# Stores of z, mixing, gated product and residual sums issued from GpSimd's queue instead of SyncE's, in a hybrid gMLP and state-space block

## The chip, the core and the metric

The kernel runs on one core of a Trainium2 chip. The metric is the device time of one execution in microseconds (us). The kernel before has a median of 2923.4 us over three runs (2920.72 to 2925.73 us).

The engines have the names of the profile: PE is TensorE (matrix products), DVE is VectorE, ACT is ScalarE, POOL is GpSimd, SP is SyncE, which computes nothing and only issues transfers. "SPq", "ACTq" and "POOLq" are rows for the instructions that an engine's sequencer carries out itself: transfers that it issues, and waits. Every engine works through its own list of instructions in order. An instruction that waits for a semaphore holds back all that stand behind it on the same engine.

## The reference

One layer of a block for 2048 latent tokens of width 1024 (and 256 context tokens, which only supply the starting states of the scans), all in fp32:

```python
hl = _rms(x) * norm1_w * (1 + sc1) + sh1
proj = hl @ w_in                                  # u, v | z, xbc, dt
xs, bm, cm = split(silu(conv5(xbc)))
y = ssd_forward(xs, dt, bm, cm) + flip(ssd_backward(...))
g = (y + xs * d_skip) * silu(z)                   # z is used here
ssd_out = _rms(g per group) * ssd_norm_w
u, v = split(gelu(proj[..., :2048]))
mixed = einsum('hts,bcshd->bcthd', gm_ws, _rms(v)) + gm_bs
gm_out = u * mixed                                # the gated product
x = x + g1 * (concat(gm_out, ssd_out) @ w_out)    # the residual sums
x = x + g2 * swiglu(_rms(x) * norm2_w * (1 + sc2) + sh2)
return _rms(x) * final_norm_w
```

## The kernel before

Tokens are the free dimension in most places: a tile is 128 partitions x 512 tokens (256 KB), `TB = 512`, and two such tiles make a block `blk` of 1024 tokens. Every matrix product is split in three fp32r products (high x high, high x low, low x high; lines 234 to 236 in the projections, 1179 to 1181 and 1309 to 1311 in the feed-forward part, which forms each product from seven half-size ones). PE writes to PSUM; three PSUM banks (`mmp`) serve the large products in turn and five (`smp`) the small ones.

Results that don't fit in SBUF go to scratch tensors in DRAM and are loaded again later: `zscr` (z after SiLU), `mscr` (the mixing result), `gmscr` (the gated product), `x2scr` (the residual sums), `hscr` (states of the backward scan), `fscr` and `r3scr` (rows that are spread over the partitions when they are loaded), `sscr` (the scan's output), `cscr`, `ascr`, `wscr` (feed-forward). In SBUF most working tiles come from one ring of 14 buffers, `tma` (`NTMA`); from the last output half on, from a ring of 14, `t2`. Whoever writes a buffer next waits until its last readers are done, and a store is such a reader until its data has landed.

Stages, with their place in the span:

- 0 to 300 us: loads, modulation parameters, the conv branch of block 1 (`xbc(1, ...)`).
- 300 to 590 us: `run` at line 1024. The main generator is `proj_v(1)`, `proj_u(1)`, `proj_z(1)`; the second one runs states of the backward scan, row statistics and parameters beside it.
- 590 to 745 us: `xbc(0, ...)`.
- 745 to 1485 us: `run` at line 1033. The main generator is `proj_z(0)`, `proj_v(0)`, `proj_u(0)`, then `out_half(1, 0)`, `out_half(0, 0)`, `out_half(0, 1)`. The second is the rest of the backward scan and `ssd_y`, which forms the scan's output for 16 chunks x 2 groups, with `SIDE = 2.61` of its steps for one main step.
- 1485 to 1612 us: `out_half(1, 1)` beside `border()` (line 1350), which prepares the operands of the feed-forward part.
- From 1612 us: `ffn1` and `ffn2` for both blocks.

A main step is: the matrix products of one 128 x 512 result (`mm3`), then `flush()`, then a few DVE and ACT instructions that make the result from PSUM, and at the end `behind(dst, src)`, which only notes down the store. `flush()` of the next main step issues it (lines 578 to 585). So each store is issued one main step after its data was asked for, behind the loads that were issued in between. There are 160 of these stores, 32 each to `zscr`, `mscr` and `gmscr` and 64 to `x2scr`, each 128 x 512 fp32, and all are issued on SP by line 584, or rather by the queue of SyncE, `DMA = nc.sync` (line 87). SP also issues all loads. ACT issues the stores of `sscr`, `r3scr` (lines 834 and 848) and part of `rec`.

The producers of the stored tiles are DVE instructions: line 698 (z), 645 (mixing), 621 (gated product), 932 (residual sums). `V` is DVE, `S` ACT, `G` POOL (line 87).

`ssd_y` uses POOL. `y_seg` loads two rows spread over the partitions (`f_load`, lines 760 and 761), then ACT (782, 784, 786) and DVE (783, 785) make the decay matrices, POOL multiplies them (787) and forms `xd` (793). `y_out` has these lines, in which DVE waits for POOL twice:

```python
            G.tensor_tensor(out=h3(h), in0=h3(h), in1=hv(tot[:, c, g * 8:g * 8 + 8]), op=ALU.mult)
            V.tensor_tensor(out=h, in0=h, in1=pS, op=ALU.add)
        V.tensor_tensor(out=ya, in0=ya, in1=yb, op=ALU.add)
        V.tensor_tensor(out=ya, in0=ya, in1=py, op=ALU.add)
        G.tensor_tensor(out=h3(yb), in0=h3(rc[:, R_X:R_X + TB]), in1=hv(row[:, 64 + g * 8:64 + g * 8 + 8]), op=ALU.mult)
        V.tensor_tensor(out=ya, in0=ya, in1=yb, op=ALU.add)
```

(lines 813 to 818). Then z is loaded (822) and multiplied in (823). Before each output half, `load_mix` (line 883) loads 2 x 8 tiles for the next one; for the scan's half it loads `r3scr` rows (line 286) first and then scales and splits the tiles on DVE (895, 898) and ACT (897). After the last output half line 1360 calls `flush()` once more; the loads of the feed-forward operands (`hl_back`, line 1130) come next, and the splits of line 1064 and 1065. `border()` uses POOL for lines 1068.

Semaphores and the order of instructions within each engine are set by the framework from the code; the order it sets isn't always that of the code.

Of the kernel before, what the change touches and what calls it, by code (L numbers as in the profile page):

```python
# [83 lines left out]
def kernel(ctx: ExitStack, tc: tile.TileContext, xT, ctxp, cc, crow, wad1, wad2, vecs, rows,  # L84
                             gmb, wall, wdt, gmw, csts, outT, dbg=None):
    nc = tc.nc
    V, S, G, PE, DMA = nc.vector, nc.scalar, nc.gpsimd, nc.tensor, nc.sync
# [493 lines left out]

    def flush():
        for dst, src in pending:
            DMA.dma_start(dst, src)
        pending.clear()

    def gelu2(ps, mk):
# [19 lines left out]
    def proj_u(blk, hs):  # L607
        for h0 in range(0, 8, 2):
            us = [unit(U_U + h0), unit(U_U + h0 + 1)]
            for j in range(2):  # L610
                ts_ = slice((blk * 2 + j) * TB, (blk * 2 + j + 1) * TB)
                for i, (hi, lo) in enumerate(us):
                    m = tmp()
                    DMA.dma_start(m[:, :TB], mscr[h0 + i][:, ts_])
                    ps = mmp()
                    mm3(ps, [(hi[:, k * P:(k + 1) * P], lo[:, k * P:(k + 1) * P], hs[j][k][:, 0, :], hs[j][k][:, 1, :]) for k in range(KT)])
                    flush()
                    if tails and (j or i):
                        tails.pop(0)()
                    t = gelu2(ps, tmp)  # L620
                    V.tensor_tensor(out=t[:, :TB], in0=t[:, :TB], in1=m[:, :TB], op=ALU.mult)
                    behind(gmscr[h0 + i][:, ts_], t[:, :TB])
                    yield

    def proj_v(blk, hs):
# [25 lines left out]
        for hh in range(2):  # L651
            us = [unit(U_V + hh * 4 + i) for i in range(4)]
            for j in range(2):
                vh = []
                ms = sml()[:, :16]
                for c in range(4):
                    ps = mmp()
                    mm3(ps, stat_terms(hs, j * 4 + c, us, 0))
                    flush()
                    v = gelu2(ps, xin)  # L660
                    sq = tmp()
                    for h in range(4):
                        S.activation(sq[:, h * P:(h + 1) * P], v[:, h * P:(h + 1) * P], AF.Square, accum_out=ms[:, c * 4 + h:c * 4 + h + 1])
                    vh.append(v)
                    if prev is not None:
                        if c == 1:
                            gate_load(prev[0], 0)
                        if c >= 2:
                            mixing(*prev, 2 * c - 4)
                        if c == 2:  # L670
                            gate_load(prev[0], 2)
                    if c < 3:
                        yield
                V.tensor_scalar(out=ms, in0=ms, scalar1=1.0 / P, scalar2=4 * EPS, op0=ALU.mult, op1=ALU.add)
                r = newton(ms, 16)
                for c, v in enumerate(vh):
                    V.tensor_tensor(out=v[:, :TB].rearrange("p (a b) -> p a b", b=P), in0=v[:, :TB].rearrange("p (a b) -> p a b", b=P),
                                    in1=bc(r[:, c * 4:c * 4 + 4].rearrange("p (a o) -> p a o", o=1), P), op=ALU.mult)
                yield
                prev = (hh, j, vh)  # L680
# [7 lines left out]
    def proj_z(blk, hs):  # L688
        for g in range(2):
            us = [unit(U_Z + g * 4 + i) for i in range(4)]  # L690
            for c in range(8):
                ps = mmp()
                mm3(ps, stat_terms(hs, c, us, 0))
                flush()
                zdone[0] += 1 - blk
                t = tmp()
                S.activation(t[:, :TB], ps, AF.Tanh, scale=0.5)
                V.scalar_tensor_tensor(out=t[:, :TB], in0=t[:, :TB], scalar=1.0, in1=ps, op0=ALU.add, op1=ALU.mult)  # L698
                behind(zscr[blk * 8 + c][:, g * TB:(g + 1) * TB], t[:, :TB])
                yield  # L700
# [758 lines left out]
```

## Time and profile before

| | us |
|---|---|
| median of three runs | 2923.4 |
| lowest, highest | 2920.72, 2925.73 |
| the profiled execution | 2923.61 |
| its span, first to last instruction | 2921.8 |
| PE busy in the span | 2803.1 |
| DVE, ACT, POOL busy in the span | 1975.6, 1274.2, 645.4 |
| mean granted TensorE clock | 0.98 of full speed |

The span is cut in 40 slices on the page, and a digit gives the busy tenths of a slice. PEclk is the granted clock in the same way; of the two levels, 2.4 and 1.2 GHz, a 9 is all or nearly all time at the upper one. In the lists, "L584" is line 584. "A <- B: 82.2, 30, 8.2" in a list of waits says that A sat idle for 82.2 us in 30 waits that B ended, the longest 8.2 us. In a timeline the columns are start, duration, engine, line, operation and tiles, a count when several alike were merged, and in brackets the idle time of the engine just before and what ended it.

### The profile page before, as it was taken

What the parts mean: (1) busy time and instruction counts of PE and PEld (TensorE: products, weight loads), DVE (VectorE), ACT (ScalarE), POOL (GpSimd) and SP (SyncE); (2) the same over time, 40 slices, a digit from 0 to 9 for tenths busy, and PEclk for the clock granted to TensorE, in tenths of its full rate; (3) what the DMA queues carried; (4) which work ended last, traced back from release to release, by engine and by line L of the source; (5) the groups of instructions that cost most, each with busy time, mean ns of one, the idle gap of its engine ahead of it and who ended that gap; (6) DMA issues with size and microseconds to landing.
All of it is one profiled execution on the core that took longest, in us unless ns stands there. A gap on an engine that the chain in (4) does not pass through costs nothing. (4 is left out here: it accounts for less than half of the span.)

```text
span 2921.8 us, 36695 instructions
## 1 busy us (share of the span) xinstructions
PE 2803.1 (96%) x12478; PEld 2242.7 (77%) x12478; DVE 1975.6 (68%) x3007; ACT 1274.2 (44%) x2361; POOL 645.4 (22%) x555
## 2 busy tenths in 40 slices
PE   7999999999999998998979899999999999999997
PEld 2788778888677776776768688888887788888886
DVE  6776866886678888678676765555876544445556
ACT  4445343344356555444443533333554333333443
POOL 3200000200032233232202444444211222221000
PEclk8999999999999999999989999999999999999998
DMA  6232567743664678787658444445775423334654
GB/s 228 89 94 78 193 226 243 252 127 91 224 187 145 185 253 269 230 268 235 211 178 282 170 156 149 165 154 181 256 249 195 133 102 101 108 109 136 224 192 162
DMA packets 296743, 528.02 MB, mean 181 GB/s; under 512 B 28998, under 2 KB 89830, under 8 KB 296556
## 3 DMA queue, kind: packets, MB, share of 16 engines
q1 hardware_dynamic: 255756, 505.48, 53.0%
q10 hardware_dynamic: 40800, 20.21, 2.4%
q8 instruction: 98, 1.61, 0.2%
q14 instruction: 89, 0.73, 0.1%
HBM read 382.94 MB, written 142.64 MB: 180 GB/s over the span
## 5 line engine op out<-in xcount | busy, mean ns | idle before, releaser
L1065 DVE TENSOR_TENSOR hl<-w,hl 128x1024 fp32r<-128x1024 f32 x286 | 372.1, 1306 | 300.8 <-ACT hl L1064 129.5
L1064 ACT CAST hl<-w 128x1024 fp32r<-128x1024 f32 x286 | 298.8, 1048 | 423.1 <-PE smp L1311 150.0
L234 PE MATMUL mmp<-actt,whi 128*128 128x512 f32 x1120 | 455.7, 407 | 13.3 <-DVE tma L932 8.7
L236 PE MATMUL mmp<-actt,wlo 128*128 128x512 f32 x1120 | 442.1, 395 | 0.0
L235 PE MATMUL mmp<-actt,whi 128*128 128x512 f32 x1120 | 441.5, 394 | 0.2 <-DVE actt L898 0.2
L1179 PE MATMUL mmp<-hl,hl 128*128 128x512 f32 x704 | 276.5, 393 | 2.6 <-ACT t L1204 2.6
L1181 PE MATMUL mmp<-hl,hl 128*128 128x512 f32 x704 | 275.7, 392 | 1.0 <-DVE hl L1065 1.0
L1180 PE MATMUL mmp<-hl,hl 128*128 128x512 f32 x704 | 275.6, 392 | 0.0
L234 PEld LDWEIGHTS mmp<-actt,whi 128*128 128x128 f32 x1120 | 213.7, 191 | 62.0 <-DVE tma L932 9.7
L235 PEld LDWEIGHTS mmp<-actt,whi 128*128 128x128 f32 x1120 | 213.8, 191 | 47.0 <-issue 4.3
L236 PEld LDWEIGHTS mmp<-actt,wlo 128*128 128x128 f32 x1120 | 213.2, 190 | 46.0 <-issue 0.2
L234 PE MATMUL mmp<-whi,actt 128*128 128x512 f32 x512 | 208.9, 408 | 2.9 <-DVE tma L698 2.9
L1180 PE MATMUL smp<-hl,hl 128*128 128x512 f32 x528 | 208.5, 395 | 3.0 <-DVE hl L1065 3.0
L1181 PE MATMUL smp<-hl,hl 128*128 128x512 f32 x528 | 208.2, 394 | 2.5 <-DVE hl L1065 2.5
L1179 PE MATMUL smp<-hl,hl 128*128 128x512 f32 x528 | 209.8, 397 | 0.4 <-ACT hl L1064 0.4
L235 PE MATMUL mmp<-wlo,actt 128*128 128x512 f32 x512 | 206.4, 403 | 0.5 <-DVE wlo L221 0.5
L236 PE MATMUL mmp<-whi,actt 128*128 128x512 f32 x512 | 206.0, 402 | 0.0
L1071 DVE TENSOR_TENSOR t<-smp,t 128x512 f32<-128x512 f32 x88 | 60.5, 687 | 181.1 <-PE smp L1181 131.4
L787 POOL TENSOR_TENSOR tma<-tma 128x512 f32<-128x512 f32 x64 | 93.4, 1461 | 339.4 <-ACT tma L786 138.4
L456 DVE SCALAR_TENSOR_TENSOR tma<-xin,cw,tma 128x512 f32<-128x512 f32 x192 | 144.3, 751 | 25.5 <-ACT tma L454 19.3
L1179 PEld LDWEIGHTS mmp<-hl,hl 128*128 128x128 f32 x704 | 132.7, 189 | 32.5 <-ACT t L1204 3.0
L1071 POOL TENSOR_TENSOR w<-w 128x512 f32<-128x512 f32 x44 | 58.9, 1339 | 446.2 <-DVE hl L1065 290.8
(276 smaller groups left out, 5809.0 us busy)
## 6 DMA issues: line engine op xcount, KB each, us to landing
w<-in_wall_dram SPq DMA_DIRECT2D x110, 512.0 KB, 3.8
ws<-in_wall_dram SPq DMA_DIRECT2D x104, 512.0 KB, 5.0
ascr<-t SPq DMA_DIRECT2D x154, 256.0 KB, 3.9
w<-ascr SPq DMA_DIRECT2D x154, 256.0 KB, 3.3
tma<-fscr SPq DMA_DIRECT2D x128, 256.0 KB, 5.7
w<-wscr SPq DMA_DIRECT2D x88, 256.0 KB, 3.0
t<-x2scr SPq DMA_DIRECT2D x76, 256.0 KB, 4.1
w<-in_wall_dram SPq DMA_DIRECT2D x66, 256.0 KB, 3.1
```

The costliest lines, as they stand in the source:

```text
L234: PE.matmul(ps, lhsT=lh, rhs=rh, start=(i == 0), stop=False)
L235: PE.matmul(ps, lhsT=lh, rhs=rl, start=False, stop=False)
L236: PE.matmul(ps, lhsT=ll, rhs=rh, start=False, stop=(i == n - 1))
L456: V.scalar_tensor_tensor(out=acc[:, :n], in0=raw[:, j:j + n], scalar=cw[:, ch, j:j + 1], in1=acc[:, :n], op0=ALU.mult, op1=ALU.add)
L787: G.tensor_tensor(out=A, in0=A, in1=fb, op=ALU.mult)
L1064: S.copy(hi, x)
L1065: eng.tensor_tensor(out=lo, in0=x, in1=hi.bitcast(F32), op=ALU.subtract)
L1071: eng.tensor_tensor(out=o, in0=a, in1=b, op=ALU.add)
L1179: PE.matmul(ps, lhsT=hi[:, ms_], rhs=t[:, 0, :], start=first and k == 0, stop=False, skip_group_check=not first)
L1180: PE.matmul(ps, lhsT=hi[:, ms_], rhs=t[:, 1, :], start=False, stop=False, skip_group_check=not first)
L1181: PE.matmul(ps, lhsT=lo[:, ms_], rhs=t[:, 0, :], start=False, stop=k == 3, skip_group_check=not first)
```

## The change

In `flush()` the queue of POOL takes the place of that of SP. Nothing else is edited:

```diff
     def flush():
         for dst, src in pending:
-            DMA.dma_start(dst, src)
+            G.dma_start(dst, src)
         pending.clear()
```

`flush()` is called at lines 617 (`proj_u`), 659 (`proj_v`), 694 (`proj_z`), 931 (`out_half`) and 1360 (after the last output half). All 160 stores go through it.

## Rows read from the trace of the kernel before

**Rows 1.** The page: busy time by engine, and the granted clock in 40 slices.
```profile
PE 2803.1 (96%) x12478; PEld 2242.7 (77%) x12478; DVE 1975.6 (68%) x3007; ACT 1274.2 (44%) x2361; POOL 645.4 (22%) x555
...
PEclk8999999999999999999989999999999999999998
```

**Rows 2.** Busy time by stretch: length, PE, PEld, DVE, ACT, POOL, clock, DMA share, GB/s.
```profile
300.00:590.00 290.00, 285.16 (x1278) 229.00 (x1277) 222.36 (x428) 111.96 (x239) 16.02 (x17) 1.00 0.69 230
...
745.00:1485.00 740.00, 695.83 (x3124) 541.49 (x3125) 582.76 (x1148) 369.72 (x983) 203.23 (x156) 0.97 0.71 222
1485.00:1612.00 127.00, 116.35 (x499) 93.80 (x498) 85.68 (x132) 54.92 (x85) 17.33 (x12) 0.96 0.74 239
```

**Rows 3.** PE's instructions at its longest waits, from the timeline of PE.
```profile
1375.23 0.65 PE L831 MATMUL smp<-ident,tma 128*128 128x128 f32 x4 [3.82 <-DVE tma L823]
1387.59 2.04 PE L801 MATMUL smp<-h,rec_sb 128*128 128x512 f32 x2 [4.64 <-issue]
...
1522.64 0.79 PE L234 MATMUL mmp<-actt,whi 128*128 128x512 f32 x1 [8.72 <-DVE tma L932]
...
1634.83 0.50 PE L1181 MATMUL smp<-hl,hl 128*128 128x512 f32 x1 [2.53 <-DVE hl L1065]
```

**Rows 4.** SP's own waits over the whole span, those of the stores of line 584.
```profile
SPq L584 <- DVE tma L932: 82.2, 30, 8.2
...
SPq L584 <- DVE tma L621: 57.3, 23, 5.1
SPq L584 <- DVE tma L698: 56.9, 17, 8.4
```

**Rows 5.** Instructions of one line (584, 787, 793): count, duration min/median/max in ns.
```profile
L584 SPq DMA_DIRECT2D x2scr<-tma x48: 319/320/1197, 1145.0 to 1523.9; - x48
...
DMA to landing us min/median/max: 2.0/3.8/7.0
...
L787 POOL TENSOR_TENSOR tma<-tma x64: 1263/1296/3148, 793.4 to 1470.4; 128x512 f32<-128x512 f32 x64
...
L793 POOL TENSOR_TENSOR tma<-rec_sb,ddt x30: 1033/1086/3194, 794.6 to 1425.0; 128x512 f32<-128x512 f32 x30
```

**Rows 6.** Timeline of SP at two stores with loads behind them.
```profile
1348.19 0.33 SPq L584 DMA_DIRECT2D x2scr<-tma  x1
1348.61 2.12 SPq L286 DMA_DIRECT2D tma<-r3scr  x4
...
1602.94 0.94 SPq L1287 DMA_DIRECT2D x2t<-x2scr  x2
1607.94 0.32 SPq L584 DMA_DIRECT2D x2scr<-t  x1
1608.30 10.73 SPq L1130 DMA_DIRECT2D t<-cscr  x16
```

**Rows 7.** Timeline of ACT: the store of the r3scr rows.
```profile
1341.66 0.38 ACTq L848 DMA_DIRECT2D r3scr<-tma  x1
```

**Rows 8.** Timeline of DVE: a residual sum; the first scaling of mixed tiles.
```profile
1201.41 0.74 DVE L932 SCALAR_TENSOR_TENSOR tma<-mmp,m_sb,tma 128x512 f32<-128x512 f32 x1
...
1353.46 6.18 DVE L895 SCALAR_TENSOR_TENSOR xin<-xin,vec,tma 128x512 f32<-128x512 f32 x8
```

**Rows 9.** Waits of ACT, DVE and SP in 745 to 1485 us.
```profile
ACT tma L782 <- DMA tma<-fscr: 85.8, 39, 5.9
...
DVE tma L783 <- ACT tma L782: 56.8, 34, 3.8
...
SPq L915 <- DMA x2scr<-tma: 10.3, 6, 5.6
```

**Rows 10.** Timeline of POOL: instructions that start right after a store's place on POOL.
```profile
820.94 1.15 POOL L793 TENSOR_TENSOR tma<-rec_sb,ddt 128x512 f32<-128x512 f32 x1
...
1203.48 1.49 POOL L813 TENSOR_TENSOR h<-h,tot 128x512 f32<-128x512 f32 x1
...
1563.20 1.28 POOL L1071 TENSOR_TENSOR w<-w 128x512 f32<-128x512 f32 x1
```

## Prediction, made before the changed kernel was run

> **What bounds the kernel now.** I read the page first: PE is busy 96% of the span and the granted clock stays near its upper level, so the ceiling of any gain is the small rest [rows 1]. Then the table by stretch, since the stores are issued only in some stages. From 300 to 590 us PE idles 290 - 285.2 = 4.8 us, from 745 to 1485 us 740 - 695.8 = 44.2 us, from 1485 to 1612 us 127 - 116.4 = 10.6 us; DVE idles 740 - 582.8 = 157.2 us in the long stretch, and POOL is busy only 203 us of it [rows 2]. Next PE's own longest waits: what ends them is mostly DVE, late with something that stands behind a batch of its work, not a transfer [rows 3]. Last the waits of SP: its stores of line 584 wait for the DVE instruction that makes their data, 82.2 + 57.3 + 56.9 = 196.4 us over the three main kinds [rows 4]. SP computes nothing, so this costs only through the loads that stand behind such a store. The question is thus which of those loads some engine needed at once, and what the same stores do in POOL's list.
>
> **What is removed.** 160 issues at 0.32 us [rows 5] are 51 us of SP's time, and the 196.4 us of waits go with them [rows 4]. Neither lies on PE's path; the loads behind do, in three places.
>
> (a) At 1348.19 us a store has just been let go, and the four loads of the r3scr rows follow at 1348.61 us [rows 6]. ACT issued the store of these rows at 1341.66 us [rows 7]; with the 2.0 to 3.8 us that the stores of line 584 take to land [rows 5] the rows are in DRAM at about 1344 to 1345.5 us. So the loads could go 3 to 4.6 us earlier, and with them DVE's batch, which starts at 1353.46 us [rows 8] and behind which PE then waits 3.8 us at 1375 and 4.6 us at 1387 us [rows 3]. Bounds 0 (DVE fills the time with other work of its list) and 4.6 us; I take 3.
>
> (b) The last store, at 1607.94 us, holds back the 16 loads of the feed-forward operands, which start at 1608.30 us; SP had been free since 1603.9 us [rows 6]. PE waits 2.5 us for a split of such an operand at 1634.8 us [rows 3]. Bounds 0 and 2.5; I take 1, since the splits have a queue of their own on ACT and DVE.
>
> (c) All through the scan ACT waits for the rows of `f_load`, 85.8 us, and DVE for ACT behind it, 56.8 us [rows 9]. Some of these loads stand behind a store. Of DVE's idle time in this stretch the share 44.2 / 157.2 = 0.28 shows up as idle time of PE [rows 2]; I use it as the rate at which a delay of DVE reaches PE. Bounds 0 and 56.8 x 0.28 = 16 us; I take a quarter of that, 4, because a load that no store holds back still waits for a free buffer.
>
> Sum of the gains: 3 + 1 + 4 = 8 us.
>
> **What is added.** POOL now issues the 160 stores, and no row shows POOL issuing a transfer. The nearest rows: SP's issue of the very same store is 0.32 us, POOL's shortest pass over a tile of this size 1.03 us, its longest 3.1 to 3.2 us [rows 5]. I take 1.0, the shortest pass, since POOL has no row on a tile below that; 0.32 and 3.15 remain as ends. The price by the Trainium skill (DMA: Bandwidth & Descriptors, Latency and other measured facts) is about 1 us to the first byte on this path against 0.6 us on the other; with it the sum would stay as it is.
>
> From 300 to 590 us POOL has next to nothing else to do (16 of 290 us [rows 2]); I cost those 48 stores at nothing. Their cover is POOL's emptiness; if it went, 48 us at most would stand ahead of the few POOL instructions there.
>
> In the other 112 a store stands in POOL's list between instructions of the scan. For each I took from the timelines the end of the DVE instruction that makes its data and of the POOL instruction ahead of it; the later of the two is where the store can go. On average that is 1.3 us after the data, SP's issue 1.0 us: POOL is in step. The wait for the data is hardly ever new, because what POOL does next depends on DVE instructions that come after it in DVE's list. What counts is POOL's next instruction: 25 times it starts within 1 us, first at 820.94 and last at 1563.20 us [rows 10]. An example: the residual sum ends at 1202.15 us [rows 8], POOL is busy until 1203.5 us, and line 813 starts at 1203.48 us [rows 10], where the store would stand. At a price of 1.0 us these pushes add up to 34 us, at 0.32 us to 19, at 2 us to 64, at 3 us to 106. Of the 34, 16 us fall on lines 813 and 817, which the next DVE instructions wait for; the others (787, 793) feed PE an item later and have slack. So 16 x 0.28 = 4 us reach PE. Ends: 0, and 106 x 0.28 = 30 us. SP's order and ACT's see none of this.
>
> A store that lands later also holds its buffer of the ring longer: by the price, about 1 us. SP's loads of residual inputs already waited 10.3 us for landings of x2scr stores in 6 cases [rows 9]; I take 1 us for this, ends 0 and 10. Loads that read back what was stored come at least a dozen main steps later, except z, which is stored tens of microseconds ahead; nothing there.
>
> **Sum.** -8 + 4 + 1 = -3 us on the profiled execution's own 2923.6 us (span 2921.8 and 1.8 around it): 2920.6 us. That execution is the median of the runs shown (2923.4) to 0.01%. About 0.2%, 5.8 us, is what a measurement of this kernel can tell from no change.
>
> **Rivals.**
>
> *Nothing moves.* The held loads are hidden, as the 157 us of DVE's idle time and the few us of PE waits ended by a transfer suggest; POOL is idle enough to take the stores. Only SP's 51 us of issue time go, which nobody waits for: 2923.5, within 2 us. The Trainium skill has this as a rule (DMA: Bandwidth & Descriptors, Issuing engines are not separate DMA queues): transfers from all queues run on the same engines, and issuing from several saves only the issue time. Against it speak places (a) and (b), where the loads start in the very instant in which the store is off. Chance 0.10.
>
> *SP's wait sets the pace of the scan.* Then (a) brings both PE waits, 8.5, (b) 2.5 and (c) its 16 us, together 27, less 5 of cost: 2901.6. For it: 85.8 us of ACT on transfers. Against: most of PE's waits end with DVE's own batches. Chance 0.18.
>
> *POOL's issue is dear and DVE waits for POOL.* This is the case on the other side. POOL's passes stretch from 1.3 to 3.1 us when others use SBUF [rows 5]; if an issue stretches likewise to 2 us, the pushes are 64 us, 18 us reach PE through lines 814 and 818, the ring adds 5 and the gains shrink to 2: +21, 2944.6. It decides once the pushes pass (8 + 6) / 0.28 = 50 us, that is a price of some 1.6 us. The Trainium skill (DMA: Bandwidth & Descriptors, SWDGE vs HWDGE vs iDMA) says that such an issue has GpSimd write descriptors into SBUF, from which VectorE can lock it out; no run so far shows that. Chance 0.25.
>
> *The order itself changes.* The framework orders each engine's list: the loads of line 1287 stand ahead of those of line 1130, which come first in the code [rows 6]. With the stores elsewhere it may place other instructions differently, and the terms above don't hold; 2910 to 2935. Chance 0.05.
>
> **The numbers.** My forecast has 0.42; its own range, with the terms between half and twice, is 2911 to 2928: 0.17 faster by over 0.2%, 0.23 within, 0.02 slower. Nothing moves: 0.10 within. Pace of the scan: 0.18 faster. Dear issue: 0.25 slower. Other order: 0.02 faster, 0.03 slower. Together 0.37, 0.33, 0.30. The range runs from the second rival's 2901.6 with a little below, 2900, to the third's 2944.6, 2945; what is left out is the dearest issue (30 + 10 us) and a gain of more than all three places.
>
> **What would show it.** Right: SP's list without waits at line 584; the loads of line 286 at about 1345 us in the old count, 3 us or more ahead of their place; those of line 1130 some 4 us earlier against the end of the last output half; POOL's next instruction about 1 us later in a sixth of the cases; PE's idle time from 745 to 1612 us down from 55 to some 50 us. Wrong: POOL rows of 2 us or more per store, or DVE waiting for POOL in lines 814 and 818 by tens of us (the third rival); ACT's wait for fscr unchanged (the first); half of it gone and PE's idle time at 35 us (the second); a list of PE or DVE in another order (the fourth).

## The result, and the profile after

The changed kernel takes 2959.7 us (median of four runs, 2948.2 to 2963.3) against 2924.4 us for the kernel before: a ratio of 1.0116, 95% interval 1.0087 to 1.0145. By the ratio that is 34 us more (25 to 42), outside the range that was given. The profiled execution took 2960.0 us, its span 2958.2. One execution each of pool_oldlists, pool_behind, act_spare and two_casts (3994 to 6698 us) was in a slow state and is left out of the medians below, not out of the 2930.25 and 2922.31 us that some expectations quote.

The page of the changed kernel, busy time by engine and the queue that is new (packets, MB, share of 16 engines):

```profile
PE 2811.9 (95%) x12478; PEld 2247.7 (76%) x12478; DVE 1995.7 (67%) x3007; ACT 1275.4 (43%) x2361; POOL 727.7 (25%) x715
...
q0 software_dynamic: 12800, 41.95, 3.6%
```

POOL has 160 instructions more than in [rows 1] and 82 us more of busy time. DVE is 20 us longer busy with the same 3007 instructions. Next the stretches. Their bounds are the times at which PE starts the same large product (the same number in its list) as at 300, 590, 745 and so on in the kernel before, so that each row answers to one of [rows 2]:

```profile
300.10:597.60 297.50, 287.67 (x1277) 230.21 (x1276) 223.49 (x429) 112.01 (x239) 40.86 (x65) 0.99 0.67 225
...
751.80:1516.90 765.10, 701.56 (x3124) 544.92 (x3125) 599.01 (x1148) 370.89 (x984) 248.13 (x248) 0.95 0.68 215
1516.90:1644.80 127.90, 116.58 (x499) 93.70 (x498) 88.39 (x130) 54.16 (x84) 30.45 (x33) 0.97 0.71 240
```

Most of the loss stands in the first two, 7.5 us and 25.1 us; the third has 0.9, and 3.4 us more come at the start of the feed-forward part. In the long stretch PE's idle time went from 44.2 to 63.5 us, and its busy time from 695.8 to 701.6 us for the same 3124 instructions, at a granted clock of 0.95 instead of 0.97. So 5.7 of the 25 us go with more time at the lower of the two levels (1.2 against 2.4 GHz). From about 1720 us on the two kernels run in step.

What the stores do on POOL: POOL's own waits, over the whole span.

```profile
POOL mscr L584 <- DVE tma L645: 167.7, 18, 72.0
POOL zscr L584 <- DVE tma L698: 136.7, 27, 28.1
...
POOL gmscr L584 <- DVE tma L621: 115.1, 24, 14.2
POOL x2scr L584 <- DVE tma L932: 104.0, 21, 23.1
```

The instructions of line 584, those of the residual sums:

```profile
L584 POOL DMA_DIRECT2D x2scr<-tma x48: 539/580/592, 1163.7 to 1553.2; - x48
...
DMA to landing us min/median/max: 2.3/4.7/9.7
```

SP's waits of [rows 4] are gone and stand on POOL. An issue takes POOL 0.54 to 0.58 us, half of what was assumed. Landing has a median of 4.7 us instead of 3.8 [rows 5]. What PE waits for, over the whole span:

```profile
PE smp L643 <- DMA gw<-in_gmw_dram: 16.4, 9, 3.8
PE mmp L234 <- DVE tma L932: 11.4, 4, 7.3
...
PE smp L831 <- DVE tma L823: 7.7, 1, 7.7
PE smp L802 <- DVE tma L807: 7.7, 1, 7.7
```

And the waits of ACT and DVE in the long stretch that answer to [rows 9], with one that has grown (2.8 us in 2 waits before):

```profile
ACT tma L782 <- DMA tma<-fscr: 96.8, 35, 11.4
...
DVE tma L783 <- ACT tma L782: 60.6, 35, 4.7
...
ACT tma L784 <- DMA x2scr<-tma: 19.6, 4, 6.7
```

No wait of tens of us stands out. Waits that were there before [rows 3, 9] are a little longer in many places, DVE hardly waits for POOL (5.0 us at line 818 in the whole span), and ACT waits longer for buffers whose store has not landed. That is the picture of a changed order, not of one late engine. The lists of the two programs say so as well. This many instructions (the stores of line 584 left out) stand at another place of their engine's list; they are counted in the programs, and a trace has somewhat more records:

```
engine     in the list   at another place   blocks of permuted instructions
PE            11857            126               22
DVE            2943            341               52
ACT            2252            185               46
POOL            555             15                6
SP             1558            198               30
```

Nothing of this is in the diff. The framework orders each list, and with the stores on another queue it ordered them otherwise. Of the 156 blocks 49 are a swap of two neighbours; the longest, on DVE, has 46 instructions.

### The profile page after: what moved, and what is told of

Same layout as the page of the kernel before. It is cut to its first block, busy times and chain, and to the rows that moved or that the text cites. A ratio compares the mean times of both kernels' runs of the same rounds, so it can differ in the third digit from the quotient of the medians.

```text
span 2958.2 us, 36954 instructions
## 1 busy us (share of the span) xinstructions
PE 2811.9 (95%) x12478; PEld 2247.7 (76%) x12478; DVE 1995.7 (67%) x3007; ACT 1275.4 (43%) x2361; POOL 727.7 (25%) x715
## 5 line engine op out<-in xcount | busy, mean ns | idle before, releaser
L1181 PEld LDWEIGHTS mmp<-hl,hl 128*128 128x128 f32 x704 | 133.2, 189 | 38.2 <-DVE hl L1065 9.7
L1179 PEld LDWEIGHTS mmp<-hl,hl 128*128 128x128 f32 x704 | 133.0, 189 | 33.0 <-ACT t L1204 2.9
```

Source lines behind the costliest of these rows:

```text
L1179: PE.matmul(ps, lhsT=hi[:, ms_], rhs=t[:, 0, :], start=first and k == 0, stop=False, skip_group_check=not first)
L1181: PE.matmul(ps, lhsT=lo[:, ms_], rhs=t[:, 0, :], start=False, stop=k == 3, skip_group_check=not first)
```

## The experiments

**Holding the lists.** A helper adds an edge from each instruction of an engine's list to the next one. The edges fix the order of issue and add no wait: put into the kernel before with that kernel's own lists, the helper gives a program with the same instructions, semaphores and waits as without it. The list can be that of the kernel before or that of the changed kernel; the 160 stores are left out of it unless said otherwise, so that the framework places them.

```diff
         tile_hybrid_block_kernel(tc, *args)
+        hold_order(nc, tc)
```
```python
for row in rows:
    last = None
    for name in row:
        if last is not None:
            tc.add_manual_dep(got[name], last, info, reason="order")
        last = name
```

| kernel | stores on | lists | median, before beside it | ratio (95%) |
|---|---|---|---|---|
| changed kernel | POOL | new | 2959.7, 2924.4 | 1.0116 (1.0087 to 1.0145) |
| pool_oldlists | POOL | old | 2928.0, 2921.0 | 1.0027 (1.0015 to 1.0039) |
| sp_newlists | SP | new | 2955.7, 2921.0 | 1.0112 (1.0095 to 1.0129) |
| pool_oldcompute | POOL | old, SP free | 2934.0, 2917.1 | 1.0047 (1.0029 to 1.0064) |
| pool_oldloads | POOL | SP old, others free | 2946.6, 2917.1 | 1.0094 (1.0075 to 1.0112) |
| weights_new | SP | old, weights new | 2942.9, 2923.4 | 1.0074 (1.0055 to 1.0094) |
| weights_old | SP | new, weights old | 2963.9, 2923.4 | 1.0140 (1.0120 to 1.0159) |
| decay_new | SP | old, decay new | 2941.1, 2923.4 | 1.0066 (1.0047 to 1.0085) |
| two_casts | SP | old, 4 moved | 2923.2, 2920.9 | 1.0011 (1.0002 to 1.0021) |
| loads_here | SP | old, 32 loads new | 2926.9, 2920.9 | 1.0022 (1.0008 to 1.0035) |
| place_387 | SP | old, one place new | 2927.5, 2920.9 | 1.0025 (1.0014 to 1.0036) |
| act_oldlists | ACT | old | 2917.9, 2923.4 | 0.9982 (0.9972 to 0.9992) |
| act_free | ACT | free | 2943.7, 2920.2 | 1.0086 (1.0067 to 1.0104) |
| pool_behind | POOL | old, 13 stores later | 2921.5, 2920.2 | 1.0006 (0.9995 to 1.0018) |
| act_spare | ACT, spare ones on POOL | old | 2920.0, 2920.9 | 0.9997 (0.9988 to 1.0007) |
| act_behind | ACT | old, 23 stores later | 2917.3, 2920.9 | 0.9989 (0.9980 to 0.9998) |

Below, a ratio is turned into us with 2921.

### Queue or order

Theories: A, the new order of the lists costs the time; B, POOL's issues and waits do. Two kernels cross them: the changed kernel with the old lists held, and the kernel before with the new lists held.

```diff
 pool_oldlists
-            DMA.dma_start(dst, src)
+            G.dma_start(dst, src)
+        hold_order(nc, tc)    rows: PE, DVE, ACT, POOL, SP of the kernel before
 sp_newlists
+        hold_order(nc, tc)    rows: PE, DVE, ACT, POOL, SP of the changed kernel
```

> Stores on POOL as in the changed kernel, but the lists of PE, DVE, ACT and SP (without the 160 stores) and POOL's arithmetic are held in the order of the kernel before; only the place of the stores in POOL's list is left to the framework. Theory A (the framework's new order of the lists costs the 36 us): most of the loss goes, 2920 to 2932 us. Theory B (POOL's issues and waits, and buffers held longer, cost it, whatever the order): 2945 to 2965 us. In between, 2932 to 2945, both have a part. In the stretch where POOL has almost nothing else (300 to 590 us of the kernel before), A expects under 2 us of loss, B the 8 us of the changed kernel.

> The reverse: the stores are on SP as before, but the lists of PE, DVE, ACT and SP (without the stores) and POOL's arithmetic are held in the order of the changed kernel; the place of the stores in SP's list is left to the framework. Theory A (order): about as slow as the changed kernel, 2945 to 2965 us. Theory B (the queue itself): about the time before, 2918 to 2930 us.

Stores on POOL in the old order cost 8 us (4 to 11); stores on SP in the new order 33 us (28 to 38). In the trace of pool_oldlists PE starts the large product of 590 us 0.8 us later than before and that of 1042 us at the same time: no loss where the changed kernel had lost 7.6 and 16.7. So A carries 26 us (34 less 8) to 33 us, and B has a part of its own; the two parts together, 41 us, lie within the interval of the 34.

### Which list

```diff
 pool_oldcompute, against pool_oldlists
-        rows: PE, DVE, ACT, POOL, SP of the kernel before
+        rows: PE, DVE, ACT, POOL of the kernel before
 pool_oldloads, against pool_oldlists
-        rows: PE, DVE, ACT, POOL, SP of the kernel before
+        rows: SP of the kernel before
```

> Stores on POOL; the lists of PE, DVE and ACT and POOL's arithmetic are held in the order of the kernel before, but SP's list is left to the framework, which then puts the loads nearly as in the changed kernel. Theory A1 (the new order of the loads on SP carries the loss): 2945 to 2960 us. Theory A2 (the new order of the arithmetic on DVE, ACT and PE carries it): 2924 to 2935 us, about as with all lists held (2930.25).

> The mirror: stores on POOL, only SP's list of loads held in the order of the kernel before; PE, DVE, ACT and POOL are left to the framework, which then orders DVE and PE much as in the changed kernel. Theory A1: 2924 to 2935 us. Theory A2: 2945 to 2960 us. If both lists matter only as a pair (each list fits the other), both this kernel and the one before it are slow.

Against all lists held (1.0027) the kernel with SP alone held is clearly slower (1.0094): the order of the arithmetic carries more (A2). With SP free the ratio is 1.0047, 6 us more but not clear of the noise, so a part of the loads is not shown by this pair.

Next, classes of instructions, with the stores back on SP: into the old lists the new places of one class are put, or the reverse.

```diff
 weights_new, against the lists of the kernel before
+        lines 217 (SP), 220 (ACT), 221 (DVE) placed as in the changed kernel
 weights_old, against the lists of the changed kernel
+        lines 217 (SP), 220 (ACT), 221 (DVE) placed as in the kernel before
 decay_new, against the lists of the kernel before
+        lines 782, 784, 786 (ACT), 783, 785 (DVE) placed as in the changed kernel
```

> Stores on SP, all lists in the order of the kernel before, except the path of the weights: SP's loads of line 217, ACT's casts of line 220 and DVE's splits of line 221 stand where the changed kernel has them (15 of 104 splits moved, up to 45 places, many ahead of a main step's own instructions). Theory W (weights put ahead of the chain of a main step, which then waits for their transfer): a third or more of the 33 us that the new lists cost on SP, so 2932 to 2942 us. Theory D (the scan's decay matrices ahead of the main step) or no single culprit: 2918 to 2928 us.

> The complement: stores on SP, all lists in the order of the changed kernel, except that the path of the weights (lines 217, 220, 221) stands where the kernel before has it. Theory W: 2935 to 2945 us, a third or more of the loss gone. Theory D or no single culprit: 2948 to 2958 us, as with all lists new (2955.69).

> Stores on SP, all lists in the order of the kernel before, except the decay matrices of the scan: ACT's lines 782, 784, 786 and DVE's 783 and 785 stand where the changed kernel has them (some 140 of DVE's 512 moved, three quarters of them ahead). Theory D (these get ahead of the residual sums and of other results of the main step, on which PE's banks wait): 2932 to 2945 us. Theory W or no single culprit: 2918 to 2928 us.

Each class by itself costs over a third of the 33 us, 22 and 19. But to put the weights' path back into the new lists doesn't gain 10 to 20 us; the kernel gets slower still, 41 us against 33. Theory W falls with that, and so does D as an only culprit: the parts don't add up. In both cases a list of which one class is moved no longer fits the others; that any class would do this is not shown.

### One place

What was open was whether such a loss is local. The changed kernel loses 8.2 us between the large products of 388 and 451 us. There the lists differ in two blocks on ACT, one of 7 instructions and two of 3 and 2 on DVE, and two blocks of loads on SP. The kernel two_casts moves two casts (line 220) and two splits (line 221) there, and nothing else; the first of each:

```diff
   ACT  L589  activate        DVE  L590
+  ACT  L220  cast            DVE  L221  split
   ACT  L591  activate        DVE  L592
                              DVE  L645, L645, L674
-  ACT  L220  cast            DVE  L221  split
```

The timeline of ACT in the kernel before:

```profile
385.16 0.60 ACT L589 ACTIVATE xin<-mmp 128x512 f32<-128x512 f32 x1 [2.30 <-PE mmp L236]
386.51 0.63 ACT L591 ACTIVATE xin<-xin 128x512 f32<-128x512 f32 x1 [0.75 <-DVE xin L590]
388.13 1.05 ACT L220 CAST whi<-ws 128x1024 fp32r<-128x1024 f32 x1 [0.99 <-DMA ws<-in_wall_dram]
```

In the changed kernel:

```profile
385.85 0.60 ACT L589 ACTIVATE xin<-mmp 128x512 f32<-128x512 f32 x1 [2.29 <-PE mmp L236]
388.93 1.05 ACT L220 CAST whi<-ws 128x1024 fp32r<-128x1024 f32 x1 [2.48 <-DMA ws<-in_wall_dram]
389.89 0.63 ACT L591 ACTIVATE xin<-xin 128x512 f32<-128x512 f32 x1
```

In two_casts:

```profile
384.95 0.60 ACT L589 ACTIVATE xin<-mmp 128x512 f32<-128x512 f32 x1 [2.30 <-PE mmp L236]
388.48 1.05 ACT L220 CAST whi<-ws 128x1024 fp32r<-128x1024 f32 x1 [2.93 <-DMA ws<-in_wall_dram]
389.43 0.63 ACT L591 ACTIVATE xin<-xin 128x512 f32<-128x512 f32 x1
```

Line 591 is a step of the main chain. It follows line 589 after 1.35 us in the kernel before, and after 4.0 and 4.5 us behind the cast, which waits for its weights. The loads have the same shape. SP's timeline in the kernel before:

```profile
387.58 0.42 SPq L277 DMA_DIRECT2D tma<-in_xT_dram  x1
...
393.65 0.33 SPq L217 DMA_DIRECT2D ws<-in_wall_dram  x1
```

In place_387, which has the new order of this place alone, on ACT, DVE and SP:

```profile
391.04 0.33 SPq L217 DMA_DIRECT2D ws<-in_wall_dram  x1
...
393.34 0.42 SPq L277 DMA_DIRECT2D tma<-in_xT_dram  x1
```

With the weights' load put first, SP stands until a weight buffer is free, and the rows of x, which ACT's line 261 needs next, go out 5.4 us later (PE itself is 0.4 us later in this run). PE's waits between 387 and 451 us in the kernel before:

```profile
424.13 1.10 PE L269 MATMUL smp<-tma,ones 128*128 128x512 f32 x2 [1.79 <-DVE tma L264]
```

In place_387:

```profile
408.03 0.50 PE L234 MATMUL mmp<-actt,whi 128*128 128x512 f32 x1 [2.13 <-DVE tma L592]
...
431.52 1.21 PE L269 MATMUL smp<-tma,ones 128*128 128x512 f32 x2 [4.30 <-DVE tma L264]
```

Line 592 belongs to the chain of 589 and 591, and line 264 takes what line 261 makes of the rows of x.

```diff
 loads_here, against the lists of the kernel before
+        13 and 19 loads of SP, at 388 to 433 us, in the order of the changed kernel
 place_387, against the lists of the kernel before
+        these, the four of two_casts, and two short blocks of DVE at 410 and 430 us
```

> Stores on SP and all lists as in the kernel before, but at one place, 387 us, two casts of weights on ACT (line 220) and two splits on DVE (line 221) stand where the changed kernel has them: the first cast ahead of line 591 and the first split ahead of line 592 of the same main step, the second cast ahead of four short squares and the second split two to five instructions earlier; nothing else moves. Theory A in its local form (an instruction put ahead that waits for its weights holds up the chain of the main step behind it, where that chain has no slack): 2 to 4 us more, all of it between 387 and 451 us, where the changed kernel lost 8. If single places don't matter and only the sum of many moves does: no change, under 1 us there.

> Stores on SP and all lists as in the kernel before, but two stretches of SP's list, 13 and 19 loads at 388 to 433 us, stand in the order of the changed kernel (the weights and four tiles of x for later steps ahead of the rows of x that ACT's line 261 needs at once). Local theory: the other part of the 8 us of this place, 3 to 6 us, between 387 and 451 us. Otherwise under 1 us.

> Both of the last two at once, with two more swaps on DVE at 410 and 430 us: all that the changed kernel orders anew in this place, on ACT, DVE and SP, and nothing elsewhere. Local theory: the 8 to 10 us that the changed kernel and sp_newlists lost between 387 and 451 us are all here, 2928 to 2932 us in all. If the loss hangs on the moves elsewhere too: under 4 us.

The local theory holds for this place. Four moved instructions cost 3 us (1 to 6), 32 loads 6 us (2 to 10), both together 7 us (4 to 11), which is a little less than the 2928 to 2932 us expected. In the traces PE loses 2.4, 7.8 and 8.6 us between these two products, the last as much as the changed kernel; decay_new, which moves nothing here, loses none (0.7 us less). The same stretch by busy time in the kernel before:

```profile
388.00:451.00 63.00, 61.21 (x285) 50.52 (x284) 42.62 (x70) 30.33 (x51) 0.00 (x0) 1.00 0.81 265
```

In the changed kernel:

```profile
388.70:459.90 71.20, 64.02 (x284) 51.69 (x284) 45.58 (x74) 32.04 (x54) 8.09 (x15) 0.98 0.74 246
```

In place_387:

```profile
388.40:460.00 71.60, 65.06 (x285) 52.92 (x284) 44.72 (x73) 31.62 (x53) 0.00 (x0) 0.95 0.76 240
```

PE's idle time, 1.8 us in the first, is 7.2 and 6.5 us in the others; the rest of the loss is busy time, 2.8 and 3.9 us more at a granted clock of 0.98 and 0.95. In the profiled run of place_387, the fastest of its twelve (2922.1 us), these 8.6 us don't all last: 3.6 us come back between 745 and 947 us and 3.5 us between 1369 and 1485 us. What gives them back is not shown. That several such places, some of them given back later, make up the 26 us is likely and not shown; only this one was taken apart.

### What the stores cost on POOL, and what SP gains

ACT's queue takes SP's waits away without POOL, the old lists held:

```diff
-            DMA.dma_start(dst, src)
+            S.dma_start(dst, src)
```

> Stores on ACT's queue, all lists (stores apart) in the order of the kernel before. It parts the 8 us that the stores on POOL cost with the lists held (2930.25). If they come from POOL (longer DVE instructions beside an issue, POOL's arithmetic later): 2916 to 2924 us, and the gain of the loads that no store holds back shows. If they come from loads that start earlier and buffers held longer: 2926 to 2935 us here too. If ACT's own waits for DVE hurt, since ACT feeds the decay matrices: over 2935 us.

It is faster than the kernel before, by 5 us (2 to 8). Where: in its trace PE is 0.1 us behind the kernel before at the large product of 1330 us and 4.4 us ahead at that of 1345 us. Between them ACT waits for rows of `f_load`, place (c), and PE for DVE. In the kernel before:

```profile
1336.23 1.28 ACT L782 ACTIVATE tma<-tma,nacs 128x128 f32<-128x128 f32 x4 [2.61 <-DMA tma<-fscr]
...
1338.71 3.65 PE L804 MATMUL smp<-rec_sb,tma 128*128 128x64 f32 x16 [3.02 <-DVE h L814]
```

In act_oldlists:

```profile
1334.85 1.28 ACT L782 ACTIVATE tma<-tma,nacs 128x128 f32<-128x128 f32 x4 [1.81 <-DMA tma<-fscr]
...
1337.33 1.97 PE L804 MATMUL smp<-rec_sb,tma 128*128 128x64 f32 x16 [1.53 <-DVE h L814]
```

The loads of these rows, which stood behind a store that left SP at 1327.57 us, go out 0.75 us earlier, line 782 starts 1.4 us earlier, and so does line 814, which stands behind line 783 in DVE's list. PE's wait halves. Its granted clock, which in the kernel before is 0.5 (1.2 GHz) from 1338.6 to 1345.4 us, behind this wait, stays at the upper level, and the 16 instructions of line 804 take 1.97 instead of 3.65 us. In the trace of act_behind, a kernel further on, PE gains as much here, from 0.5 us behind to 4.3 ahead.

Place (a) gives hardly any of it. Its loads, in the row of line 286 (count, duration, first and last start), start at 1344.3 us instead of 1348.61 [rows 6], when PE is ahead already:

```profile
L286 SPq DMA_DIRECT2D tma<-r3scr x8: 319/354/399, 1344.3 to 1492.1; - x8
```

DVE's batch behind them starts only 1.6 us earlier, for in both kernels DVE is busy with other lines up to then. From 1345 to 1400 us, past the two waits of [rows 3], PE gains 0.4 us.

So on POOL the stores cost 8 + 5 = 13 us more than on ACT. A part is a wait. POOL's timeline in the kernel before:

```profile
1228.95 1.05 POOL L817 TENSOR_TENSOR hb<-rec_sb,row 128x512 f32<-128x512 f32 x1 [1.25 <-PE mmp L236]
1233.07 1.05 POOL L813 TENSOR_TENSOR h<-h,tot 128x512 f32<-128x512 f32 x1 [3.08 <-PE smp L801]
```

In pool_oldlists:

```profile
1191.23 0.58 POOL L584 DMA_DIRECT2D x2scr<-tma  x1 [1.37 <-DVE tma L783]
1191.83 1.06 POOL L813 TENSOR_TENSOR h<-h,tot 128x512 f32<-128x512 f32 x1
...
1237.71 1.04 POOL L817 TENSOR_TENSOR hb<-rec_sb,row 128x512 f32<-128x512 f32 x1 [1.26 <-PE mmp L236]
1244.12 0.58 POOL L584 DMA_DIRECT2D x2scr<-tma  x1 [5.36 <-DVE tma L932]
1244.72 1.06 POOL L813 TENSOR_TENSOR h<-h,tot 128x512 f32<-128x512 f32 x1
```

Line 813 follows 817 after 3.1 us in the first, as soon as PE's line 801 has read the state; in the second after 6.0 us, because a store in between waits for its residual sum. In 13 places from 745 to 1612 us POOL waited for a store's data, 40 us together, and its arithmetic started right behind. The next kernel swaps these 13 stores with the instruction behind them:

```diff
   POOL  L817
-  POOL  L584  x2scr
   POOL  L813
+  POOL  L584  x2scr
```

> As pool_oldlists (stores on POOL, all other lists as in the kernel before, 2930.25 us), but in POOL's list 13 of the 160 stores change places with the one POOL instruction behind them: those of the stretch from 745 to 1612 us before which POOL sat waiting for the store's data (0.6 to 7.3 us each, 40 us together in that trace) and behind which its arithmetic started at once. Theory P1 (POOL's arithmetic is held back by the wait of a store ahead of it, and DVE and PE behind it): most of the 13 us between this place of the stores and ACT's queue (2917.86) goes, 2918 to 2924 us. Theory P2 (the issues themselves, with longer DVE instructions beside them, and later landings): 2927 to 2932 us, since every issue stays.

The ratio falls from 1.0027 to 1.0006, by 6 us (1 to 11): P1 for about half of the 13. In its timeline line 813 follows after 4.2 us and the store stands behind:

```profile
1231.50 1.05 POOL L817 TENSOR_TENSOR hb<-rec_sb,row 128x512 f32<-128x512 f32 x1 [1.25 <-DVE tma L815]
1236.73 1.04 POOL L813 TENSOR_TENSOR h<-h,tot 128x512 f32<-128x512 f32 x1 [4.18 <-PE smp L801]
1237.72 0.58 POOL L584 DMA_DIRECT2D x2scr<-tma  x1
```

For the rest, the issue alone:

```diff
+    for i in range(160):
+        G.dma_start(spare[i], ones[:, 0:16])
```

> Stores on ACT's queue and all lists held, as in act_oldlists (2917.86 us, ratio 0.9982), and POOL's list besides issues 160 spare stores of 128 x 16 elements (64 B per partition, of a tile that is never rewritten, into a scratch tensor that nobody reads), in the very places where pool_behind (2922.31 us, ratio 1.0006) issues the real ones. Their data are always there and no buffer hangs on them, so what they cost is the issue alone. Theory P2 in its remaining part (the issue on POOL, with POOL's time and the longer DVE instructions beside it): ratio 1.000 to 1.002, all or most of the 7 us between the two. If the rest lies in landings and buffers held: ratio 0.997 to 0.9985, no cost.

It issues 160 transfers more than the computation needs. 0.9997 lies between the two marks: 160 issues on POOL that wait for nothing cost 4 us against act_oldlists (0.9982), 2 against act_behind (0.9989), the latter not clear of the noise. They also go earlier than the real ones, the first at 253.7 us instead of 324.5, since nothing holds them. So the issues are a part of the remaining 7 us; how large it is, and whether the buffers of the ring have one, stays open.

```diff
 ACT, one of the 23 places
-  ACT  L584  x2scr
   ACT  L786
+  ACT  L584  x2scr
```

> As act_oldlists, but 23 stores in ACT's list, before which ACT sat waiting for the store's data for 0.3 to 6.9 us (40 us together) and behind which its next instruction started at once, change places with that one instruction. If a wait of a store in the list of an engine that computes costs as much here as on POOL: 2 to 5 us less than act_oldlists, ratio 0.9965 to 0.9975. If ACT has slack at these places: ratio 0.998 to 0.9985.

0.9989 is no gain over 0.9982, if a little outside both marks: ACT has slack there, which POOL hadn't. It is a second kernel whose interval lies below 1, so the gain of some 3 to 5 us with the stores on ACT is not one run's luck.

```diff
 act_free, against act_oldlists
-        hold_order(nc, tc)
```

> Stores on ACT's queue, no list held: the framework orders all of them anew, as it did in the changed kernel. Theory A in its general form (a new order costs some tens of us whatever queue it comes from, because the order before was the better one): 2935 to 2960 us. If only the order that comes with POOL is bad: 2912 to 2925 us, as with the lists held (2917.86).

Without held lists the same edit is 25 us slower than the kernel before. The new order that comes with ACT costs 30 us, about as much as that of POOL: the loss isn't peculiar to POOL's order, and of these three orders the old one is the best.

## Why the prediction was wrong

**The step that failed** is the premise that the lists stay as they are ("SP's order and ACT's see none of this"). The whole sum rested on it and put a new order at nothing; the fourth rival, "The order itself changes", gave it a chance of 0.05 and 2910 to 2935 us. The sign that the framework places instructions by its own rule was in [rows 6] and was named; its price was not worked out from anything. The runs show 26 to 33 us there, most of the 34. Rows of before would have given a wider bound: the waits of [rows 3], 2.5 to 8.7 us each, are of PE behind an instruction that stood behind others, and a new order may make such a wait elsewhere, as it did at 387 us.

**The gains**, forecast as 8 us, are 5 with ACT's queue, net of what the stores cost there. (a), forecast as 3 within 0 to 4.6, is 0.4: the prediction took DVE's batch at 1353.46 us for one that waits for the loads, and DVE has no pause before it from 1347.4 us on, which is the case it had named for its lower bound. (b) was forecast as 1 and is nothing: from 1612 to 1680 us, where it should show, the lead stays at 4.4 to 4.5 us. (c), forecast as 4, gives the 4.5 us at 1330 to 1345 us, but not as it was argued: not by a rate over the whole scan, but at one wait, and two thirds of it through the clock, which the sum did not count. That 8 and 5 are near each other is luck in part. In the changed kernel none of it shows: its r3scr loads start here, by SP's timeline:

```profile
1374.85 5.26 SPq L286 DMA_DIRECT2D tma<-r3scr  x4
```

That is 1348.8 us in the old count (PE is 26 us late there), not earlier than before, and ACT's wait for fscr rose from 85.8 to 96.8 us instead of falling.

**The price of an issue** was taken as 1.0 us and is 0.54 to 0.58; its effect, forecast as 4 us, was measured as 2 to 4 with act_spare. The figure of the Trainium skill that stood beside it (DMA: Bandwidth & Descriptors, Latency and other measured facts) is for the first byte, and no row here is of that.

**The step "the wait for the data is hardly ever new"** failed too. It said that POOL's next instruction depends on DVE instructions that come later anyhow. Line 813 depends on PE's line 801, and 13 times POOL's arithmetic was ready while a store ahead of it waited; that is 6 us. It was argued from an average (1.3 us against SP's 1.0), which hid these cases. The prediction's own pushes spoke against it: 19 us at a price of 0.32 and 34 at 1.0 lie on a line that leaves some 12 us at no price at all.

**The rivals.** The dear issue had the right sign and 21 of the 34 us (2944.6), but not the mechanism: no issue took 2 us, and lines 814 and 818 don't wait for POOL by tens of us. Its sum also let all 64 us of pushes reach DVE where the forecast had let 16 of 34; by the same share it would have had some 8 us in place of 18. SP's wait doesn't set the pace of the scan. The rule of the Trainium skill behind "Nothing moves" (DMA: Bandwidth & Descriptors, Issuing engines are not separate DMA queues) says that another issuing engine saves only the time of the issue; act_oldlists agrees in that the gain is small, 5 us, but its gain stands where loads no longer wait behind a store's data, at 1329 us, and not in the 51 us of issues.

**Of the signs that the prediction listed against itself**, ACT's wait for fscr, which didn't fall, and the lists in another order came; issues of 2 us and a DVE that waits for POOL didn't. From 745 to 1612 us PE's idle time went from 55 to 75 us instead of 50.

## What to carry to other kernels

Where a framework orders the lists, an edit of one queue can be an edit of every list: compare the lists of both programs before reading any wait, and hold the old order to see what the edit itself does. In an order that fits, an instruction that waits costs time when it is put ahead of one that others need at once: a load on SP, a cast on ACT, a store on POOL. Four instructions moved cost 3 us here. Stores belong to an engine with slack: here ACT's queue with the order held gained 5 us where POOL's lost 8.

## What the runs showed of the hardware

A store lands no later from POOL's queue than from ACT's in the median, 4.7 us from both (the changed kernel and act_oldlists), against 3.8 from SP [rows 5]; the longest landings are 9.7 and 6.4 us. An issue on POOL by itself doesn't lengthen a DVE instruction: in pool_oldlists 15 instructions of line 783 that overlap only an issue take 0.346 us in the mean, 189 that overlap nothing of POOL 0.345. But of nine in lines 783 and 785 that start beside an issue with POOL's arithmetic next in line, seven last to the end of that arithmetic, 1.59 to 1.69 us; beside the other two it is POOL's own line 787 that takes 3.1 us. DVE's timeline of pool_oldlists, four instructions at a time:

```profile
1190.85 2.46 DVE L783 SCALAR_TENSOR_TENSOR tma<-tma,acs 128x128 f32<-128x128 f32 x4
...
1241.93 1.23 DVE L783 SCALAR_TENSOR_TENSOR tma<-tma,acs 128x128 f32<-128x128 f32 x4 [1.73 <-ACT tma L782]
```

The second group is undisturbed. In the first, one of the four starts at 1191.37 us, during the issue at 1191.23 us shown above, and ends at 1193.04 us, just behind line 813, which runs from 1191.83 to 1192.89 us: 1.67 us instead of 0.345. Undisturbed it would have ended 0.1 us before line 813 began; why it was held already is not shown. The Trainium skill (SBUF — State Buffer, Who interferes with whom) says that a DVE instruction with two inputs in SBUF contends with a POOL instruction that reads SBUF, and calls the port pair that they share an exclusive lock. These rows agree. In the kernel before, where POOL issues nothing, the longest instruction of line 783 took 1.40 us; in pool_oldlists one took 2.16 us with no issue near it, beside two POOL instructions in a row. The same section says that a transfer stalled by a DVE instruction is one that POOL issued; the median landing shows none of that here, and the longest ones, 9.7 us against 6.4, leave it open.
